# Where the bias table fills stand in an encoder layer: from the windowed attention into the first FFN's gate/up blocks

## The chip, the cores and the metric

The kernel runs on one core of a Trainium2 chip. The metric is the device time of one execution in microseconds (us). The kernel before takes 2405.37 us, the median of three runs (2403.84 to 2407.05).

## The reference

One encoder layer with two half-step SwiGLU FFNs around a mixing layer. The mixing layer has two kinds of heads: A, windowed grouped-query attention with rotary embedding (rope), and B, a neighbourhood attention on a token grid, whose scores get a learned relative position bias from the table `rpb_b`, and minus infinity (-1e30) where a key lies outside the neighbourhood. There are 1024 sample tokens and 256 prompt tokens, D_MODEL = 1024, D_FF = 2816.

```python
def swiglu(x, w_gu, w_down):
    g, u = jnp.split(x @ w_gu, 2, axis=-1)
    return (jax.nn.silu(g) * u) @ w_down
...
def encoder_layer(x, ffn1_pre, ffn1_w_gu, ffn1_w_down, ffn1_post, mix_pre, w_in, sink_a, rpb_b,
                  out_norm_a, out_norm_b, w_out, mix_post, ffn2_pre, ffn2_w_gu, ffn2_w_down, ffn2_post, final_norm):
    B, S, _ = x.shape
    x = x + 0.5 * rmsnorm(swiglu(rmsnorm(x, ffn1_pre), ffn1_w_gu, ffn1_w_down), ffn1_post)
    h = rmsnorm(x, mix_pre)
    proj = h @ w_in
    qa, ka, va, qb, kb, vb = jnp.split(proj, np.cumsum([D_A, D_KV_A, D_KV_A, D_B, D_B]), axis=-1)
    qa = rope(qa.reshape(B, S, N_HEADS_A, HEAD_DIM))
    ka = rope(ka.reshape(B, S, N_KV_A, HEAD_DIM))
    va = va.reshape(B, S, N_KV_A, HEAD_DIM)
    oa = window_gqa(qa, ka, va, sink_a)
    ob = neighbourhood_attn(qb.reshape(B, S, N_HEADS_B, HEAD_DIM), kb.reshape(B, S, N_HEADS_B, HEAD_DIM),
                            vb.reshape(B, S, N_HEADS_B, HEAD_DIM), rpb_b)
    mix = jnp.concatenate([rmsnorm(oa, out_norm_a), rmsnorm(ob, out_norm_b)], axis=-1) @ w_out
    x = x + rmsnorm(mix, mix_post)
    x = x + 0.5 * rmsnorm(swiglu(rmsnorm(x, ffn2_pre), ffn2_w_gu, ffn2_w_down), ffn2_post)
    return rmsnorm(x, final_norm)
```

## The kernel before

**Stages.** The 1280 tokens are 10 tiles of 128. The stages follow one another on TensorE: gate/up of the first FFN (to about 608 us), its down product (to about 900 us), the input projections, attention A, attention B, the output projection, the second FFN, the final norm. Every product is made of three matmuls over a high and a low part of each operand (`ah`, `al` for weights; `xh`, `xl` for activations).

**Gate/up** is in class `GateUp`. D_FF is cut into NFF = 22 blocks of 128, HF = 11 in each half. A block f is 14 steps: 7 products over a chunk of 256 columns and 7 over a chunk of 384, the 7 being the products of a Strassen scheme, each with its own weight operand. Step n is number n of these 14. `run(f)` issues the steps of block f, and between them `prep(f + 1)`, which makes the seven operand pairs A(f+1) (`ah` on ScalarE, L69; `al` and the sums `s` on VectorE, L72 and L249 to L258) from the raw weights. At its end `load(f + 2)` (L229) loads the raw weights raw(f+2), two loads of 512 KB, on SP's queue. The raw tiles have two buffers, so one pair: raw(f+2) needs raw(f+1) to have been used up. The results `w` and `v` of a block are stored to HBM on ACT's queue (`store`, L319) and, in the second half, the planes of the first half are read back by `fetch` (L326) on SP's queue. `weight_sums` loads `bx` and `bt` of the down weights (L396 to L401) on SP, adds them on GpSimd (POOL) and stores them (`td0T`) on ACT's queue.

**Bias tables.** `bias_tables` makes the tables `tt` and `ttp` in HBM that attention B reads as `tab`. A *skew* loads `cm` (L538), adds rows of `rpb_b` to it on GpSimd (`z`) and stores it to the scratch tensors `zd` and `zp` (L544). `fill_neg` writes 512 KB of minus infinity to `ttp` (L564). A *fill* is one HBM to HBM DMA `tt<-zd` of 384 KB (L552) and one or two DMAs `tt<-in_neg_dram` of 48 to 192 KB (L557), whose source is one short row of minus infinity read for every row of the target. `fill_p` is four DMAs `ttp<-zp` (L560). There are six skews, 16 fills and four `fill_p`. In the kernel before, hook 6 of blocks 2 to 10 takes the first nine pieces (six skews, the first fill, then two fills at a time), tied behind the last raw weight load by `issue_after`; the rest goes as the list `fills` to attention A, where `pinned` ties each behind the latest rope swap.

**Attention A** runs four groups j of heads. While group j runs, the queries of group j+1 are projected and go through `rope`: the projection is copied to `qf`, four DMAs on SP's queue swap its halves into `qs` (L709), and `qf`, `qs` are multiplied and added (L711 to L714). The scores need the split operand of it (`stk`).

**Order.** The instructions of each engine, and the DMAs of each queue, run in the order of the built program; a scheduler sets this order at build, within the ties of `issue_after`. A DMA also waits until the DMA that last used its completion semaphore has landed; eight such semaphores go round among the DMAs of SP and ACT.

Of the kernel before, what the change touches and what calls it, by code (L numbers as in the profile page):

```python
# [32 lines left out]
HF = NFF // 2  # L33
# [133 lines left out]
class GateUp:  # L167
# [8 lines left out]
    def __init__(self, c, tc, w_gu, wp, G, hd):  # L176
        self.c, self.tc, self.wp, self.G, self.hd = c, tc, wp, G, hd
        self.w = w_gu.rearrange("(k p) (s f) -> p k s f", p=128, s=2)
        self.xb = [[None] * 7 for _ in CHUNKS]
        self.A, self.raw, self.back, self.later, self.held, self.last_v = {}, {}, {}, [], [], []  # L180
        self.work = None

# [41 lines left out]
    def load(self, f):  # L224
        if f < NFF:
            self.raw[f] = []
            for s in range(2):
                r = self.wp.tile([128, 8, 128], F32, name="raw", bufs=2)
                self.last_load = self.c.nc.sync.dma_start(r, self.w[:, :, s, f * 128:(f + 1) * 128])  # L229
                self.raw[f].append(r)  # L230
# [90 lines left out]
    def fetch(self, f, ch):  # L321

        n = CN[ch]
        x = self.back[f, ch] = self.G.tile([128, 2 * n], F32, name="back", tag="x", bufs=3)
        with self.tc.issue_after(self.last_load.ins):
            self.c.nc.sync.dma_start(x.rearrange("p (r x) -> p r x", x=128), self.plane(("w0", "v0"), f, ch))  # L326

# [18 lines left out]
    def steps(self, f):  # L346
        k = "01"[f >= HF]

        def step(ch, j):
            self.product(f, ch, j)  # L350
            if j == 0:
                self.queued(self.last_v)
            if j == 4:
                self.queued(self.later)
# [163 lines left out]
def bias_tables(c, G, rpb, cmask, neg, tt, ttp, zd, zp):  # L518
# [4 lines left out]
    nc = c.nc  # L523
# [44 lines left out]
    fills = [lambda a=a, rh=rh: fill(a, rh) for a in range(8) for rh in range(2)][1:]  # L568
    while len(first) < HF - 2:
        two, fills = fills[:2], fills[2:]  # L570
        first.append(lambda two=two: [f() for f in two])
    return first, fills + [lambda a=a: [fill_p(a, n) for n in range(4)] for a in range(4)]

# [27 lines left out]
def mix_attention(c, tc, xt, w_in, sink, cosT, sinT, maskA, tt, ttp, oAd, oBd, mw, L, R,  # L601
                  close_left, open_out, late, mr, pre, fills):
    nc = c.nc
# [98 lines left out]
    def rope(th, ps, store):  # L702
# [5 lines left out]
        for b in range(4):  # L708
            state["pin"] = nc.sync.dma_start(qs[b * 32:b * 32 + 32], qf[(b ^ 1) * 32:(b ^ 1) * 32 + 32])  # L709
        yield  # L710
# [38 lines left out]
    qA = {}  # L749
# [211 lines left out]

    def pinned(f):
        with tc.issue_after(state["pin"].ins):
            f()

    with in_order(tc, mybir.EngineType.DVE):
# [11 lines left out]
    for j in range(4):  # L978
        units = [[(att_A(j, t), ATT)] for t in range(NT)]
        if j < 3:  # L980
            todo = P(("qA", j + 1))
            for n in range(7):
                if fills:
                    todo.insert(4 * n + 3, (0.0, lambda f=fills.pop(0): pinned(f)))
            pipe.run(units, todo)
        else:
            pipe.run(units + [[]] * 5, P(("qkB", 0), ("vB", 1)))
# [183 lines left out]
def encoder(tc, i, out_p, out_s):  # L1171
# [206 lines left out]
    gu.load(2)  # L1378
    late, later = bias_tables(c, G, i["rpb_b"][0], i["cmask"], i["neg"], tt, ttp, zd, zp)

    def behind():
        with tc.issue_after(gu.last_load.ins):
            late.pop(0)()

    for f in range(1, NFF):
        gu.run(f, block_hooks(gu, f, {6: behind} if 1 < f < HF else {}, f // 2 if f == 1 or f % 2 == 0 else None))
    L.close(2)
# [30 lines left out]
    def finish1(t, x, gain, halves, ss):  # L1418
# [7 lines left out]
        if "xt" in state:  # L1426
# [7 lines left out]
            else:  # L1434
# [9 lines left out]
    mix_attention(c, tc, state["xt"], i["w_in"][0], i["sink_a"], i["cosT"], i["sinT"], i["maskA"], tt, ttp, oAd, oBd,  # L1444
                  mw, L, R, lambda: L.close(4), mo.open, lambda: [list(x) for x in state["late"]], state["mr"], state["pre"], later)
    c.ps.use(y=(2, 3, 4, 5), tr=(6, 7, 0, 1))
# [64 lines left out]
    def finish2(t, x, gain, halves, ss):  # L1511
# [8 lines left out]
        for h in (a, b):  # L1520
            nc.scalar.dma_start(rows(ys, yp, t)[:, h], x[:, h])

# [53 lines left out]
```

## Time and profile before

The profiled execution took 2403.19 us; its span, from the first to the last instruction, is 2401.4 us.

| | before |
|---|---|
| median of three runs | 2405.37 us |
| the profiled execution | 2403.19 us |
| its span | 2401.4 us |
| PE (TensorE) busy | 2273.8 us, 95% |
| VectorE, ScalarE, POOL busy | 1458.6, 982.4, 709.0 us |
| mean granted TensorE clock | 0.977 of full speed |
| HBM traffic | 372.47 MB, mean 155 GB/s |

The profile's rows name an engine, a line of the kernel, an operation and out<-in by the program's names. SPq and ACTq are the queues on which these engines issue DMAs. A row of waits says which engine waited at which line for which instruction: us in total, times, longest. The granted clock is the share of full speed at which TensorE ran. The busy share is 95% over the whole span, so it has to be read stage by stage.

### The profile page before, as it was taken

What the parts mean: (1) busy time and instruction counts of PE and PEld (TensorE: products, weight loads), DVE (VectorE), ACT (ScalarE), POOL (GpSimd) and SP (SyncE); (2) the same over time, 40 slices, a digit from 0 to 9 for tenths busy, and PEclk for the clock granted to TensorE, in tenths of its full rate; (3) what the DMA queues carried; (4) which work ended last, traced back from release to release, by engine and by line L of the source; (5) the groups of instructions that cost most, each with busy time, mean ns of one, the idle gap of its engine ahead of it and who ended that gap; (6) DMA issues with size and microseconds to landing.
All of it is one profiled execution on the core that took longest, in us unless ns stands there. A gap on an engine that the chain in (4) does not pass through costs nothing. (4 is left out here: it accounts for less than half of the span.)

```text
span 2401.4 us, 36895 instructions
## 1 busy us (share of the span) xinstructions
PE 2273.8 (95%) x13328; PEld 2072.3 (86%) x13328; DVE 1458.6 (61%) x2575; ACT 982.4 (41%) x2043; POOL 709.0 (30%) x812
## 2 busy tenths in 40 slices
PE   6999999999999999878999989899999999999997
PEld 5999999999788787657898878789999999978876
DVE  7666656655545763548665656566666656544585
ACT  5322222222434543547665655342322222243454
POOL 6121125444000123436443334622213332300022
PEclk9999999999999999878999999899999999999999
DMA  4466656666656653334433445435455655555574
GB/s 135 119 155 158 153 144 195 188 184 185 208 188 192 221 184 107 73 77 85 111 106 93 123 156 176 155 114 164 139 172 157 185 145 159 149 189 183 191 230 157
DMA packets 417094, 372.47 MB, mean 155 GB/s; under 512 B 69200, under 2 KB 339408, under 8 KB 416912
## 3 DMA queue, kind: packets, MB, share of 16 engines
q1 hardware_dynamic: 286224, 278.87, 39.5%
q10 hardware_dynamic: 130688, 91.25, 12.4%
q8 instruction: 105, 1.72, 0.3%
q14 instruction: 77, 0.63, 0.1%
HBM read 249.85 MB, written 121.90 MB: 155 GB/s over the span
## 5 line engine op out<-in xcount | busy, mean ns | idle before, releaser
L280 PE MATMUL gups<-xh,ah 128*128 128x256 f32 (+1 forms) x2464 | 764.9, 311 | 18.6 <-DVE v L289 13.5
L280 PE MATMUL gups<-xh,al 128*128 128x256 f32 (+1 forms) x2464 | 762.1, 310 | 0.0
L280 PE MATMUL gups<-xl,ah 128*128 128x256 f32 (+1 forms) x2464 | 761.8, 309 | 0.0
L462 PE MATMUL dps<-wd,hh 128*128 128x512 f32 x1540 | 482.4, 394 | 7.9 <-ACT hh L69 7.9
L280 PEld LDWEIGHTS gups<-xh,ah 128*128 128x128 f32 x2464 | 466.7, 189 | 24.5 <-DVE v L289 15.8
L280 PEld LDWEIGHTS gups<-xl,ah 128*128 128x128 f32 x2464 | 467.3, 190 | 0.0
L280 PEld LDWEIGHTS gups<-xh,al 128*128 128x128 f32 x2464 | 466.9, 190 | 0.0
L462 PEld LDWEIGHTS dps<-wd,hh 128*128 128x128 f32 x1540 | 290.9, 189 | 70.3 <-ACT hh L69 9.8
L462 PE MATMUL dps<-wd,hl 128*128 128x512 f32 x770 | 304.2, 395 | 6.6 <-DVE hl L72 6.2
L69 ACT ACTIVATE ah<-s 128x512 fp32r<-128x512 f32 x176 | 111.3, 632 | 244.4 <-PE gups L280 165.9
L72 DVE TENSOR_TENSOR al<-s,ah 128x512 fp32r<-128x512 f32 x176 | 145.0, 824 | 98.1 <-ACT ah L69 97.4
L69 ACT ACTIVATE hh<-hl 128x768 fp32r<-128x768 f32 (+1 forms) x140 | 110.6, 791 | 209.6 <-DMA hl<-hd0s 55.3
L72 DVE TENSOR_TENSOR hl<-hl,hh 128x768 fp32r<-128x768 f32 (+1 forms) x140 | 124.6, 891 | 106.3 <-ACT hh L69 106.3
L462 PEld LDWEIGHTS dps<-wd,hl 128*128 128x128 f32 x770 | 145.8, 189 | 44.2 <-DVE hl L72 12.6
L659 POOL TENSOR_TENSOR sb<-sb,rc 128x384 f32<-128x384 f32 (+1 forms) x160 | 126.1, 810 | 158.0 <-DVE rc L657 144.3
L636 PE MATMUL pj<-xh,mh 128*128 128x512 f32 (+1 forms) x432 | 162.9, 378 | 0.3
L636 PE MATMUL pj<-xh,ml 128*128 128x512 f32 (+1 forms) x432 | 156.8, 363 | 0.1
L636 PE MATMUL pj<-xl,mh 128*128 128x512 f32 (+1 forms) x432 | 156.3, 362 | 0.0
L306 ACT ACTIVATE u<-u 128x256 f32<-128x256 f32 x88 | 41.5, 472 | 253.4 <-DVE u L289 208.9
L69 ACT ACTIVATE ah<-raw 128x512 fp32r<-128x512 f32 x132 | 83.4, 632 | 138.4 <-PE gups L280 131.5
L72 DVE TENSOR_TENSOR wd<-rawd,wd 128x512 fp32r<-128x512 f32 x154 | 106.2, 692 | 47.0 <-ACT wd L69 46.5
L162 POOL TENSOR_SCALAR rs<-ssq 128x1 f32<-128x1 f32 x20 | 12.5, 624 | 396.1 <-ACT junk L479 396.1
(183 smaller groups left out, 3680.4 us busy)
## 6 DMA issues: line engine op xcount, KB each, us to landing
raw<-in_ffn_w_gu_dram SPq DMA_DIRECT2D x88, 512.0 KB, 4.1
rawd<-in_ffn_w_down_dram SPq DMA_DIRECT2D x66, 256.0 KB, 3.3
bx<-in_ffn_w_down_dram SPq DMA_DIRECT2D x22, 512.0 KB, 5.1
bt<-in_ffn_w_down_dram SPq DMA_DIRECT2D x44, 256.0 KB, 4.8
rawd<-td0T SPq DMA_DIRECT2D x44, 256.0 KB, 3.2
rawd<-td1T SPq DMA_DIRECT2D x44, 256.0 KB, 3.2
tab<-tt SPq DMA_DIRECT2D x24, 384.0 KB, 3.8
hl<-hd0s SPq DMA_DIRECT2D x20, 384.0 KB, 3.2
```

What stands on the lines that cost most here:

```text
L69: nc.scalar.activation(hi, src, AF.Copy)
L72: (lo_eng or nc.vector).tensor_tensor(lo, src, hi.bitcast(F32), op=ALU.subtract)
L162: nc.gpsimd.tensor_scalar(r, sums[0], sums[1] if len(sums) == 2 else 0.0, EPS, op0=ALU.add, op1=ALU.add)
L280: nc.tensor.matmul(ps, w[:, k, :], x[:, k, :], start=new and k == 0 and m == 0, stop=k == 3 and m == 2, skip_group_check=not new)
L306: self.last_act = nc.scalar.activation(X["u"], X["u"], AF.Silu)
L462: nc.tensor.matmul(ps, a[:, k, :], b, start=i == 0 and v == 0, stop=i == HF - 1 and v == 2)
L636: state["mm"] = nc.tensor.matmul(ps[:, :n], w[:, kk, :], xs[th][:, kk, :], start=first, stop=last)
L659: nc.gpsimd.tensor_tensor(s, s, rc[:, i:i + 1].to_broadcast(list(s.shape)), op=ALU.mult)
```

## The change

Four things change.

1. All pieces of the bias tables are queued in the first FFN: hooks 6 and 12 of blocks 2 to 10 take a piece each, none is left for attention A, and `pinned` goes.
2. A read-back by `fetch` now also counts as the last load, and each raw weight load is tied behind the last load, so raw loads are queued behind the values read back.
3. The queued stores of `later` are issued at step 5, not 4, of a chunk.
4. The output stores of the last norm go on SP's queue, not ACT's.

```diff
@@ GateUp.load
-                self.last_load = self.c.nc.sync.dma_start(r, self.w[:, :, s, f * 128:(f + 1) * 128])
+                with self.tc.issue_after(self.last_load.ins) if self.last_load else nullcontext():
+                    self.last_load = self.c.nc.sync.dma_start(r, self.w[:, :, s, f * 128:(f + 1) * 128])
@@ GateUp.fetch
-            self.c.nc.sync.dma_start(x.rearrange("p (r x) -> p r x", x=128), self.plane(("w0", "v0"), f, ch))
+            self.last_load = self.c.nc.sync.dma_start(x.rearrange("p (r x) -> p r x", x=128), self.plane(("w0", "v0"), f, ch))
@@ GateUp.steps
-            if j == 4:
+            if j == 5:
                 self.queued(self.later)
@@ bias_tables
     fills = [lambda a=a, rh=rh: fill(a, rh) for a in range(8) for rh in range(2)][1:]
-    while len(first) < HF - 2:
+    fills += [lambda a=a: [fill_p(a, n) for n in range(4)] for a in range(4)]
+    while fills:
         two, fills = fills[:2], fills[2:]
         first.append(lambda two=two: [f() for f in two])
-    return first, fills + [lambda a=a: [fill_p(a, n) for n in range(4)] for a in range(4)]
+    return first
@@ mix_attention
-            todo = P(("qA", j + 1))
-            for n in range(7):
-                if fills:
-                    todo.insert(4 * n + 3, (0.0, lambda f=fills.pop(0): pinned(f)))
-            pipe.run(units, todo)
+            pipe.run(units, P(("qA", j + 1)))
...
     def behind():
-        with tc.issue_after(gu.last_load.ins):
-            late.pop(0)()
+        if late:
+            with tc.issue_after(gu.last_load.ins):
+                late.pop(0)()
 
     for f in range(1, NFF):
-        gu.run(f, block_hooks(gu, f, {6: behind} if 1 < f < HF else {}, f // 2 if f == 1 or f % 2 == 0 else None))
+        gu.run(f, block_hooks(gu, f, {6: behind, 12: behind} if 1 < f < HF else {}, f // 2 if f == 1 or f % 2 == 0 else None))
@@ finish2
         for h in (a, b):
-            nc.scalar.dma_start(rows(ys, yp, t)[:, h], x[:, h])
+            nc.sync.dma_start(rows(ys, yp, t)[:, h], x[:, h])
```

**SP's queue in the first FFN.** Before, this is all that stands from the raw pair of block 10 (first row) to that of block 11 (last row):

```order
L229 DMA raw<-in_ffn_w_gu_dram 128x8x128 x2
L552 DMA tt<-zd 16x24x256
L557 DMA tt<-in_neg_dram 16x24x128
L552 DMA tt<-zd 16x24x256
L557 DMA tt<-in_neg_dram 16x24x128
L229 DMA raw<-in_ffn_w_gu_dram 128x8x128 x2
```

Now this stands between the raw pair of block 7 and that of block 8 (line numbers of the changed kernel are one to two higher; `x2` is two such DMAs):

```order
L553 DMA tt<-zd 16x24x256
L558 DMA tt<-in_neg_dram 16x24x32
L558 DMA tt<-in_neg_dram 16x24x96
L553 DMA tt<-zd 16x24x256
L558 DMA tt<-in_neg_dram 16x24x128
L397 DMA bx<-in_ffn_w_down_dram 128x1024
L401 DMA bt<-in_ffn_w_down_dram 128x512
L402 DMA bt<-in_ffn_w_down_dram 128x512
L553 DMA tt<-zd 16x24x256
L558 DMA tt<-in_neg_dram 16x24x64 x2
L553 DMA tt<-zd 16x24x256
L558 DMA tt<-in_neg_dram 16x24x128
```

Four fills stand there in place of two at most. Between raw pairs 8 and 9 there are again four fills with six `tt<-in_neg_dram`, without `bx` and `bt`; between 9 and 10 four fills with six, and `bx`, `bt`, `bt`; between 6 and 7 three `tt<-zd` and three `tt<-in_neg_dram`; between 10 and 11 one fill with one and twelve of the sixteen `ttp<-zp`. Of the skews, two stand in blocks 2, 3 and 4 each, where before one stood in blocks 2 to 7.

**VectorE at the edge of a block.** Before, at the edge of blocks 7 and 8 (`128x384` is the last chunk of block 7, `128x256` the first of block 8):

```order
L72 TENSOR_TENSOR al<-s_2632,ah 128x512
L303 TENSOR_TENSOR w<-w,g 128x384
L289 TENSOR_TENSOR u<-u,gups 128x384
L72 TENSOR_TENSOR al<-raw,ah 128x512
L249 TENSOR_TENSOR s_2880<-raw 128x512
L307 TENSOR_TENSOR v<-v,u 128x384
L250 TENSOR_TENSOR s_2881<-s_2880,raw 128x512
L289 TENSOR_TENSOR u<-u,gups 128x256
```

Now, at the same edge:

```order
L290 TENSOR_TENSOR u<-u,gups 128x384
L308 TENSOR_TENSOR v<-v,u 128x384
L72 TENSOR_TENSOR al<-raw,ah 128x512
L250 TENSOR_TENSOR s_2652<-raw 128x512
L251 TENSOR_TENSOR s_2653<-s_2652,raw 128x512
L72 TENSOR_TENSOR al<-s_2653,ah 128x512
L72 TENSOR_TENSOR al<-raw,ah 128x512
L255 TENSOR_TENSOR s_2653<-raw,s_2653 128x512
L72 TENSOR_TENSOR al<-s_2652,ah 128x512
L290 TENSOR_TENSOR u<-u,gups 128x256
```

Before, the first operand of A(9) and two of its sums stood there, and A(8), whose last row is the first one shown, had been made among the products of block 7. Now all of A(8) from its first operand on stands behind block 7's products, and four of the seven ahead of block 8's first product (`u<-u,gups 128x256` reads that).

**SP's queue in attention A**, for j = 1, before and now:

```order
L709 DMA qs<-qf 32x512 x4
L799 DMA oAd<-st 64x2x128
L552 DMA tt<-zd 16x24x256
L557 DMA tt<-in_neg_dram 16x24x32
L557 DMA tt<-in_neg_dram 16x24x96
L799 DMA oAd<-st 64x2x128
L552 DMA tt<-zd 16x24x256
L557 DMA tt<-in_neg_dram 16x24x128
L709 DMA qs<-qf 32x256 x4
```

```order
L711 DMA qs<-qf 32x512 x4
L801 DMA oAd<-st 64x2x128 x2
L711 DMA qs<-qf 32x512 x3
L801 DMA oAd<-st 64x2x128
L711 DMA qs<-qf 32x512
```

The rope swaps `qs<-qf` follow one another with only the small stores `oAd<-st` between.

More of the change, by code (lines that the diff above doesn't have):

```diff
@@ L1 @@
 import math
-from contextlib import contextmanager
+from contextlib import contextmanager, nullcontext
 import numpy as np
@@ L180, in __init__ @@
         self.A, self.raw, self.back, self.later, self.held, self.last_v = {}, {}, {}, [], [], []
-        self.work = None
+        self.work = self.last_load = None
     def open_chunk(self, ch, pool):
@@ L601, in mix_attention @@
 def mix_attention(c, tc, xt, w_in, sink, cosT, sinT, maskA, tt, ttp, oAd, oBd, mw, L, R,
-                  close_left, open_out, late, mr, pre, fills):
+                  close_left, open_out, late, mr, pre):
     nc = c.nc
@@ L708, in rope @@
         for b in range(4):
-            state["pin"] = nc.sync.dma_start(qs[b * 32:b * 32 + 32], qf[(b ^ 1) * 32:(b ^ 1) * 32 + 32])
+            nc.sync.dma_start(qs[b * 32:b * 32 + 32], qf[(b ^ 1) * 32:(b ^ 1) * 32 + 32])
         yield
@@ L960, in P @@
         return out
-    def pinned(f):
-        with tc.issue_after(state["pin"].ins):
-            f()
     with in_order(tc, mybir.EngineType.DVE):
@@ L1378, in encoder @@
     gu.load(2)
-    late, later = bias_tables(c, G, i["rpb_b"][0], i["cmask"], i["neg"], tt, ttp, zd, zp)
+    late = bias_tables(c, G, i["rpb_b"][0], i["cmask"], i["neg"], tt, ttp, zd, zp)
     def behind():
-        with tc.issue_after(gu.last_load.ins):
-            late.pop(0)()
+        if late:
+            with tc.issue_after(gu.last_load.ins):
+                late.pop(0)()
     for f in range(1, NFF):
-        gu.run(f, block_hooks(gu, f, {6: behind} if 1 < f < HF else {}, f // 2 if f == 1 or f % 2 == 0 else None))
+        gu.run(f, block_hooks(gu, f, {6: behind, 12: behind} if 1 < f < HF else {}, f // 2 if f == 1 or f % 2 == 0 else None))
     L.close(2)
@@ L1444, in encoder @@
     mix_attention(c, tc, state["xt"], i["w_in"][0], i["sink_a"], i["cosT"], i["sinT"], i["maskA"], tt, ttp, oAd, oBd,
-                  mw, L, R, lambda: L.close(4), mo.open, lambda: [list(x) for x in state["late"]], state["mr"], state["pre"], later)
+                  mw, L, R, lambda: L.close(4), mo.open, lambda: [list(x) for x in state["late"]], state["mr"], state["pre"])
     c.ps.use(y=(2, 3, 4, 5), tr=(6, 7, 0, 1))
```

## The prediction

> **What bounds the kernel now.** I read first the table of stretches (each row: from and to, length, then busy us of PE, PEld, DVE, ACT and POOL with instructions, then PE's granted clock, the DMA share and GB/s), because a busy share over the whole span hides where TensorE stands still.
>
> ```profile
> 77.00:322.00 245.00, 244.66 (x1681) 244.32 (x1680) 152.25 (x251) 68.71 (x130) 38.29 (x29) 1.00 0.59 148
> 322.00:608.00 286.00, 272.96 (x1845) 269.43 (x1844) 169.77 (x272) 74.26 (x143) 124.26 (x109) 0.99 0.64 185
> 956.00:1116.00 160.00, 122.45 (x606) 99.89 (x605) 93.93 (x257) 85.91 (x228) 71.88 (x126) 0.82 0.35 79
> 1116.00:1380.00 264.00, 261.08 (x1637) 231.45 (x1636) 174.20 (x485) 174.01 (x467) 109.23 (x161) 1.00 0.39 105
> ```
>
> Row 1 is blocks 1 to 10 of the first FFN's gate/up stage, 168 matmuls each, so 24.46 us a block: TensorE is full, at full clock, and nothing can be gained there, only lost. Row 3 is attention A for j = 0 to 2, the one stage where TensorE is starved: 37.6 us idle, and a clock of 0.82 in the rest. Row 4, the rest of the attention, is full again.
>
> Then the waits of the engines, in those two stages (us in total, times, longest). The first row is TensorE's only wait in row 1 above; the other three are in row 3.
>
> ```profile
> PE gups L280 <- DVE v L289: 0.3, 1, 0.3
> PE o_ps L792 <- DVE st L687: 14.2, 8, 3.6
> PE s_ps L665 <- DVE stk L72: 12.9, 7, 3.3
> ACT stk L69 <- DVE qf L714: 26.1, 10, 5.1
> ```
>
> In attention A the scores (`s_ps`) wait for `stk`, ScalarE waits for `qf` before it can make `stk`, and `qf` needs `qs`, the rotated half that the rope fetches by a DMA on SP's queue. So I looked at that queue where a bias fill stands ahead of a rope swap. First the timeline of SP (start, issue time, instruction), then the DMA view of single issues (KB each, us from issue to landing).
>
> ```profile
> 1011.77 0.60 SPq L552 DMA_DIRECT2D tt<-zd  x1
> 1012.41 1.28 SPq L557 DMA_DIRECT2D tt<-in_neg_dram  x2
> 1014.46 0.60 SPq L552 DMA_DIRECT2D tt<-zd  x1
> 1015.11 0.62 SPq L557 DMA_DIRECT2D tt<-in_neg_dram  x1
> 1015.82 10.09 SPq L709 DMA_DIRECT2D qs<-qf  x4
> ...
> tt<-zd SPq DMA_DIRECT2D x1, 384.0 KB, 4.0
> tt<-in_neg_dram SPq DMA_DIRECT2D x1, 48.0 KB, 8.9
> tt<-in_neg_dram SPq DMA_DIRECT2D x1, 144.0 KB, 13.8
> tt<-zd SPq DMA_DIRECT2D x1, 384.0 KB, 13.8
> tt<-in_neg_dram SPq DMA_DIRECT2D x1, 192.0 KB, 17.9
> qs<-qf SPq DMA_DIRECT2D x1, 32.0 KB, 17.4
> qs<-qf SPq DMA_DIRECT2D x3, 32.0 KB, 1.8
> ```
>
> Issue plus landing gives the chain: 1015.8 (table rows from `zd`), 1021.3 (fill with minus infinity, 48 KB), 1026.9 (144 KB), 1028.3 (`zd`, 384 KB), 1033.0 (192 KB), 1033.2 (the swap). The reader is to see two things. The queue lands in order, so the swap took 17.4 us where three others with no fill ahead (issued at 961 us) took 1.8. And a `tt<-in_neg_dram` **holds the queue for 4.7 to 5.6 us whatever its size**, while a `tt<-zd` with up to eight times the bytes takes 1.4. The fill's source is one row read over and over. I use 5.3 and 1.4.
>
> **The change: attention A loses its fills.** Busy 122.45 us at clock 0.82 is 100.4 us of work at full speed, so 160 - 100.4 = 59.6 us is all that this stage can give. What it keeps is read from two 20 us stretches: the stage's first, and the first of j = 3, which runs attention A without fills and without rope.
>
> ```profile
> 956.00:976.00 20.00, 16.78 (x76) 13.44 (x75) 16.65 (x41) 13.27 (x33) 11.68 (x18) 0.83 0.26 69
> 1016.00:1036.00 20.00, 11.69 (x58) 8.94 (x58) 10.18 (x29) 8.78 (x23) 7.61 (x14) 0.72 0.26 77
> 1116.00:1136.00 20.00, 19.11 (x113) 15.47 (x113) 17.53 (x50) 16.44 (x46) 14.18 (x27) 0.97 0.43 96
> ```
>
> The start stays 20 us: its 16.78 x 0.83 = 13.9 us of work waits for the first softmax chains as well. The other 86.5 us of work at the pace of j = 3 (19.11 / 20 x 0.97 = 0.927) take 93.3 us. So 160 becomes 113.3: **a gain of 46.7 us**. From above it is bounded by 59.6. From below: if only the waits of `s_ps` go (12.9 of the 37.6 us idle), and with them as large a share of the 22.1 us that the low clock costs (122.45 - 100.4), it is 12.9 + 7.6 = 20.5.
>
> **The change: the fills go to blocks 5 to 10 of the first FFN.** On DVE, ACT and POOL they cost nothing, since a fill is DMA alone. On SP they stand between two pairs of raw weight loads. The sixteen fills are 16 `tt<-zd` and 22 `tt<-in_neg_dram`. By the order shown above, six of the latter stand between raw(7) and raw(8), six up to raw(9) and six up to raw(10); the kernel before has at most three between two pairs. The rows of a stretch with one or two fills in the kernel before:
>
> ```profile
> 271.53 0.58 SPq L552 DMA_DIRECT2D tt<-zd  x1
> 272.54 0.56 SPq L557 DMA_DIRECT2D tt<-in_neg_dram  x1
> 307.31 0.62 SPq L557 DMA_DIRECT2D tt<-in_neg_dram  x1
> 307.97 3.09 SPq L396 DMA_DIRECT2D bx<-in_ffn_w_down_dram  x1
> ...
> tt<-zd SPq DMA_DIRECT2D x1, 384.0 KB, 4.5
> tt<-in_neg_dram SPq DMA_DIRECT2D x1, 192.0 KB, 8.8
> tt<-in_neg_dram SPq DMA_DIRECT2D x1, 192.0 KB, 14.0
> bx<-in_ffn_w_down_dram SPq DMA_DIRECT2D x1, 512.0 KB, 15.1
> ```
>
> `zd` lands at 276.0 and the fill behind it at 281.3: 5.3 us here too. The other fill lands at 321.3 and `bx`, 512 KB, at 323.1: 1.7 us for a plain load of that size, so 3.4 for a pair of raw loads and about the same, 3.4, for `bx` with its two halves `bt`. The stretches then take, on the queue alone:
> raw(7) to raw(8): 6 x 5.3 + 4 x 1.4 + 3.4 + 3.4 = 44.2 us; raw(8) to raw(9): 6 x 5.3 + 4 x 1.4 + 3.4 = 40.8; raw(9) to raw(10): 44.2. Against three blocks of 24.46 that is 19.7 + 16.3 + 19.7 = **55.7 us**.
>
> Is there cover? There is one pair of raw buffers, so raw(f+2) is loaded only after A(f+1) has been made from raw(f+1). Below are SP's waits from 77 to 345 us.
>
> ```profile
> SPq L229 <- DVE s L258: 69.5, 10, 18.8
> SPq L538 <- DMA td0T<-bt: 36.3, 4, 12.3
> SPq L229 <- DVE al L72: 23.1, 9, 3.2
> SPq L544 <- POOL z L542: 22.0, 5, 5.0
> SPq L557 <- DMA hd0w<-w: 9.1, 1, 9.1
> SPq L552 <- DMA hd0w<-w: 8.8, 1, 8.8
> ```
>
> SP waits 69.5 + 23.1 us over some eleven pairs, 8.4 us a block, for the raw buffer: that idle time hides what stands between the loads today. It would shorten the first long stretch. I do not subtract it from the sum, because of the last two rows: a fill waits until the DMA that used its completion semaphore before has landed, here a store of products by ACT. With four fills per block many wait for stores of the very block that they run beside, and the queue stands empty meanwhile. The cover stays in the lower bound, 55.7 - 8.4 = 47.
>
> The skews before the fills double up too: two in one block where one stood. Each costs SP about 9.1 us (36.3 / 4) at L538 and 4.4 (22.0 / 5) at L544; two are 27 us in a block of 24.46, and with the raw loads 30.4. In two such blocks (4 and 5) that is 2 x 6 = 12 us, less a little of the cover: 11, between nothing and 27 (one added skew in each, uncovered).
>
> Behind a wait of 15 to 20 us the clock is low: 0.72 in the stretch from 1016 us, that is 5.6 us of 20. While the queue sets the pace this is hidden; for block 10, behind which it no longer does, I take 4 us (0 to 6). The Trainium skill ("TensorE: Matmul & The Clock Gate", section "What's actually happening") says that the clock is halved after an idle window of about 3.4 us and restored after as long a busy one; by it one such wait would cost about 1.7 us, an estimate from that page, in place of my 4, and the sum would be 2 us less.
>
> Sum of the first FFN: 11 + 55.7 + 4 = **+71 us**, from 47 (skews and clock at nothing) to 27 + 55.7 + 6 + 6 = 95, the last 6 for stores that the queue waits for.
>
> Behind the cover stands one more lateness, which DVE's order shows: the seven operands of A(f+1) stand at the edge of the block, behind block f's own work, and the first step of the block waits for them.
>
> **The change: the rest.** In four blocks of the second half and in one of FFN2 the first of the two raw loads now stands behind `back`, not ahead of it. The place where that is longest:
>
> ```profile
> 469.87 0.38 SPq L229 DMA_DIRECT2D raw<-in_ffn_w_gu_dram  x1
> 474.80 0.38 SPq L326 DMA_DIRECT2D back<-hd0w  x1
> ```
>
> That raw load goes out 4.9 us later or less, and the second one no later. The idle 13 us of that stage (286.00 - 272.96) are not waits for raw weights, so nothing is won; what is lost I put at +1 (0 to 4.9, one full delay). The hook moved from j = 4 to 5 leaves every order as it was: 0. The output stores on SP's queue in place of ACT's: 20 stores of 256 KB beside other loads, in a stage where TensorE is busy 263.69 of 268 us:
>
> ```profile
> 2120.00:2388.00 268.00, 263.69 (x1136) 214.21 (x1137) 160.13 (x231) 124.28 (x222) 23.07 (x34) 0.99 0.62 198
> ```
>
> The stores free some time of ACT's queue and may hold up a weight load behind them; the stage's idle 4.3 us bounds a gain, a like amount a loss: 0 +- 4.
>
> **Sum.** The profiled execution took 2403.2 us (span 2401.4 and 1.8 around it). 2403.2 + 71 + 1 - 46.7 = 2428.5. It lies 2.2 below the median of the runs, 2405.4, so in those terms I say **2430 us**.
>
> **The rivals.**
> (a) *The fills are hidden beside TensorE.* Row 1 has a DMA share of 0.59, so there is room, if a fill in a full queue costs what its bytes do: by `bx` (1.7 us for 512 KB) 0.2 to 0.6 us, and no stretch exceeds 12.4 + 6 x 0.6 = 16 us. It decides at (24.46 + 8.4 - 12.4) / 6 = 3.4 us per fill: below that, nothing is lost. Only the gain would be left: 2405.4 - 46.7 + 1 = **2360 us, faster**. Against it: four fills in two stages took 4.7 to 5.6 us, with queued loads right behind. The Trainium skill ("DMA: Bandwidth & Descriptors", section "Measured (HBM→SBUF, 128 partitions, SWDGE, issued from GpSimd)") has 0.95 us for 64 KB and 6.15 for 1 MB, an estimate of 1.6 for 192 KB and so of 22 for a stretch, which would side with (a); the trace, with 5.3 us, differs. Chance 0.10.
> (b) *Both bounds meet*: loss 47 and gain 50 to 59.6, so 2394 to 2403. Speaks for it that the cover is real. Chance 0.08.
> (c) *Attention A is held by the rope itself.* `o_ps` waits 14.2 us for `st`, not for a swap; if only the 12.9 us of `s_ps` are gained, the time is 2405.4 + 72 - 12.9 = **2464 us**. Against it: j = 3 and the 1.8 us swaps. Chance 0.12.
> (d) *The change doesn't do what it says*: the scheduler could leave fills in the attention. SP's order there shows none. Chance 0.
>
> **How the numbers follow.** The forecast has 0.70, between 2404 and 2462 with its terms. The range takes in (b) and (c) and leaves (a) out: 2394 to 2466. A measurement of this kernel can tell about 0.2%, 4.8 us, from no change. Faster: (a) and half of (b), 0.14. Within: the other part of (b) and the forecast's lower edge, 0.07. Slower: 0.79.
>
> **What would show it.** In the changed profile, blocks 7 to 9 should last 40 to 45 us each, with TensorE waiting at their start for `ah` or `al` made from raw weights, raw landings of 10 us and more, and six fills landing 5 us apart ahead of each pair. Attention A to j = 2 should last about 113 us at a clock over 0.9, its swaps landing in about 2 us. I am wrong if the FFN's blocks stay at 24.5 us, or if the swaps are fast and the scores still wait for `stk`.

## The result, and the profile after

| | before | after |
|---|---|---|
| median of four runs | 2404.61 us (2402.42 to 2407.05) | 2438.09 us (2434.73 to 2443.76) |
| ratio, with its 95% interval | | 1.0141 (1.0119 to 1.0163) |
| the profiled execution, its span | 2403.19, 2401.4 us | 2439.03, 2437.3 us |
| blocks 7, 8, 9 of the first FFN together | 73.3 us | 138.4 us |
| start of block 11 | 322.5 us | 408.9 us |
| first FFN's down product, first to last matmul | 282.2 us | 283.0 us |
| attention A, first to last score | 195.1 us | 137.0 us |

The change costs 1.4%. The forecast was 2430, within 2394 to 2466. A block starts here with its first `gups` matmul in the trace.

The windows of the changed kernel, columns as in the prediction (from and to, length, PE, PEld, DVE, ACT, POOL busy, clock, DMA share, GB/s). Rows 1 to 4 are blocks 7 to 10, row 5 is attention A:

```profile
241.40:282.80 41.40, 25.25 (x169) 24.27 (x168) 14.66 (x27) 6.96 (x14) 5.22 (x4) 0.87 0.43 119
282.80:327.20 44.40, 27.95 (x169) 27.21 (x169) 13.98 (x26) 6.43 (x13) 0.00 (x0) 0.81 0.37 97
327.20:379.80 52.60, 28.03 (x168) 27.08 (x168) 14.20 (x25) 6.43 (x13) 5.35 (x4) 0.76 0.51 122
379.80:408.90 29.10, 28.39 (x169) 27.95 (x170) 13.99 (x26) 5.91 (x12) 0.00 (x0) 0.85 0.61 122
1047.00:1187.00 140.00, 133.61 (x841) 116.88 (x840) 125.12 (x357) 115.81 (x323) 104.74 (x180) 0.98 0.28 60
```

The three blocks hold the same 168 matmuls as ever, in 41 to 53 us: TensorE stands still for a third to a half of each and restarts at a low clock. In attention A it is now busy for 133.6 of 140 us at 0.98. The DMA share falls where the loss is (0.43 and 0.37 beside 0.59 before): the transfers are not short of bandwidth, something keeps them from being issued or from landing.

The waits of the changed kernel say what (engine, line, waited for: us, times, longest). The first row is TensorE's and the middle ones SP's, from 78 to 410 us; the last row is TensorE's in attention A:

```profile
PE gups L281 <- ACT ah L69: 57.2, 6, 21.8
...
SPq L230 <- DMA td0T<-bt: 30.7, 2, 16.6
SPq L558 <- DMA hd0w<-w: 18.8, 2, 13.6
SPq L230 <- DMA hd0w<-w: 16.1, 1, 16.1
SPq L553 <- DMA hd0w<-v: 13.8, 1, 13.8
...
PE s_ps L667 <- DVE stk L72: 3.4, 2, 2.4
```

TensorE waits 57.2 us for `ah`, the first operand of the next block. SP has two kinds of trouble: transfers that land slowly, and waits for stores by ACT (`td0T<-bt`, `hd0w<-w`, `hd0w<-v`: the four rows in the middle, 79.4 us) that must land before a DMA gets its completion semaphore. In the forecast's sum the second kind stands at nothing, with 6 us in its upper bound; what such a wait costs is not its length, as block 8 shows. Scores hardly wait for `stk` any more: 3.4 us where it was 12.9.

Both kinds are seen in block 8. First SP's timeline (start, issue time, instruction) of the changed kernel, then its DMA view of single issues there (KB, us to landing):

```profile
289.00 0.55 SPq L558 DMA_DIRECT2D tt<-in_neg_dram  x1
303.36 0.54 SPq L553 DMA_DIRECT2D tt<-zd  x1
303.94 0.63 SPq L558 DMA_DIRECT2D tt<-in_neg_dram  x1
...
310.29 17.12 SPq L230 DMA_DIRECT2D raw<-in_ffn_w_gu_dram  x2
...
tt<-in_neg_dram SPq DMA_DIRECT2D x1, 192.0 KB, 15.7
tt<-zd SPq DMA_DIRECT2D x1, 384.0 KB, 4.8
tt<-in_neg_dram SPq DMA_DIRECT2D x1, 192.0 KB, 9.2
raw<-in_ffn_w_gu_dram SPq DMA_DIRECT2D x1, 512.0 KB, 16.2
```

SP issues nothing from 289.6 to 303.4: the wait of 13.8 us for the store `hd0w<-v` above. But the queue does not run dry meanwhile: the 192 KB issued at 289.00 land only at 304.7, 15.7 us after their issue, behind four DMAs issued from 283.6 on. The `zd` of 303.36 lands at 308.2, the 192 KB of minus infinity behind it at 313.1 (4.9 us later), and so on until the first raw load, issued at 310.3, lands at 326.5. Block 9 starts at 327.2.

By the issue and landing times of all its DMAs, SP's queue has nothing under way for 2.5 of the 138.4 us of the three blocks. So the work on the queue sets their pace, as the forecast had it. An estimate of what a wait of SP costs there is the restart of the queue: the `tt<-zd` issued at 258.2, with nothing ahead of it, landed after 3.6 us, where one behind others takes 1.4 by the prediction's chain.

Where the 35.9 us between the spans come from, by the block and stage starts of the two traces: block 6 starts 16.7 later (skews; 1.4 of it stand already at block 1), blocks 7 to 9 take 65.0 more, block 10 takes 4.6 more, block 11 to the down product 2.9 more, the down product 0.8 more; attention A takes 58.1 less; FFN2's down product and the tail take 3.4 more. That is 35.3, so nothing large is missing.

### The profile page after: what moved, and what is told of

Read it like the earlier page. It is cut to its first block, busy times and chain, and to the rows that moved or that the text cites. A ratio compares the mean times of both kernels' runs of the same rounds, so it can differ in the third digit from the quotient of the medians.

```text
span 2437.3 us, 36888 instructions
## 1 busy us (share of the span) xinstructions
PE 2263.7 (93%) x13328; PEld 2068.8 (85%) x13328; DVE 1447.9 (59%) x2575; ACT 975.1 (40%) x2043; POOL 714.0 (29%) x812
## 5 line engine op out<-in xcount | busy, mean ns | idle before, releaser
L281 PEld LDWEIGHTS gups<-xh,ah 128*128 128x128 f32 x2464 | 473.3, 192 | 98.8 <-ACT ah L69 63.4
L281 PEld LDWEIGHTS gups<-xh,al 128*128 128x128 f32 x2464 | 473.1, 192 | 1.9 <-DVE al L72 1.9
L281 PEld LDWEIGHTS gups<-xl,ah 128*128 128x128 f32 x2464 | 473.8, 192 | 0.0
L72 DVE TENSOR_TENSOR al<-s,ah 128x512 fp32r<-128x512 f32 x176 | 139.3, 791 | 107.1 <-ACT ah L69 106.1
L307 ACT ACTIVATE u<-u 128x256 f32<-128x256 f32 x88 | 41.4, 471 | 290.2 <-DVE u L290 236.5
L403 POOL TENSOR_TENSOR bt<-bt,bx 128x512 f32<-128x512 f32 x22 | 30.3, 1377 | 419.4 <-DMA bt<-in_ffn_w_down_dram 352.3
```

Of the source, the lines that this page charges most:

```text
L72: (lo_eng or nc.vector).tensor_tensor(lo, src, hi.bitcast(F32), op=ALU.subtract)
L281: nc.tensor.matmul(ps, w[:, k, :], x[:, k, :], start=new and k == 0 and m == 0, stop=k == 3 and m == 2, skip_group_check=not new)
L307: self.last_act = nc.scalar.activation(X["u"], X["u"], AF.Silu)
L403: e(b22, b22, b12, op=sub)
```

## The experiments

Every kernel ran beside the kernel before on the same chip; a ratio is against those runs. Lengths are from the profiled execution of each, which lies up to 7.7 us from the median of its kernel.

| kernel | median us | ratio (95%) | blocks 7-9 | block 11 starts | down product | attention A |
|---|---|---|---|---|---|---|
| fills_only | 2438.48 | 1.0146 (1.0123 to 1.0169) | 137.2 | 411.0 | 284.9 | 134.9 |
| rest_only | 2413.09 | 1.0029 (1.0016 to 1.0042) | 73.8 | 325.5 | 287.4 | 193.6 |
| skews_only | 2423.23 | 1.0072 (1.0055 to 1.0090) | 73.9 | 341.5 | 284.0 | 195.0 |
| after_own_rows | 2409.63 | 1.0014 (1.0005 to 1.0023) | 99.8 | 379.0 | 284.8 | 135.2 |
| before_own_rows | 2409.06 | 1.0009 (1.0000 to 1.0018) | 73.4 | 325.4 | 284.3 | 191.9 |
| fills_in_down | 2390.26 | 0.9934 (0.9910 to 0.9959) | 73.4 | 323.4 | 321.9 | 137.1 |
| small_copies_in_A | 2393.84 | 0.9945 (0.9930 to 0.9960) | 73.8 | 323.7 | 325.4 | 137.3 |
| large_copies_in_A | 2461.80 | 1.0228 (1.0213 to 1.0244) | 73.4 | 324.5 | 324.3 | 205.3 |
| fills_in_A_written_order | 2400.43 | 0.9970 (0.9959 to 0.9981) | 73.3 | 323.5 | 283.2 | 183.3 |
| fills_in_down_wider | 2380.23 | 0.9887 (0.9872 to 0.9902) | 74.1 | 323.6 | 314.9 | 136.9 |
| small_copies_in_ffn | 2404.97 | 0.9991 (0.9979 to 1.0004) | 74.4 | 328.8 | 313.5 | 136.0 |
| large_copies_in_ffn | 2457.10 | 1.0208 (1.0190 to 1.0225) | 101.4 | 373.2 | 310.1 | 135.8 |

### Which part of the change costs

`fills_only` is the kernel before with the bias pieces moved and nothing else of the change (the lists of `bias_tables`, hooks 6 and 12, no `pinned`).

> The kernel before with the fills' part of the change alone (all pieces in blocks 2 to 10, none in attention A); raw loads, output stores and the hook at step 4 as before. Theory (the fills make the loss of the first FFN and the gain of attention A; raw order and output stores cost about 3 us each): the first FFN's gate/up stage ends 84 to 88 us later than before, attention A is 56 to 60 us shorter, together 2404.6 + 27 to 30 = 2431 to 2435 us. Rival (the raw loads tied behind the read-back make a good part of the loss): below 2425 us.

`rest_only` is the other half: the raw loads tied behind `back`, `later` at step 5, the output stores on SP.

> The kernel before with everything of the change but the fills: raw loads behind the read-back, the hook at step 5, output stores on SP's queue. Theory: the first FFN's second half is about 3 us longer, the last down product and the tail about 3 us: 2404.6 + 4 to 8 = 2409 to 2413 us. Rival (these edits cost nothing by themselves, the 3 us came from the shifted state after the fills): 2403 to 2406 us.

`skews_only` doubles only the skews, in blocks 2 to 4; the later hooks are as before.

```diff
-        gu.run(f, block_hooks(gu, f, {6: behind} if 1 < f < HF else {}, ...
+        gu.run(f, block_hooks(gu, f, ({6: behind, 12: behind} if 1 < f < 5 else {6: behind} if 7 < f < HF else {}), ...
```

> The kernel before with one thing of the change: the six skews stand two to a block in blocks 2 to 4 (hooks 6 and 12) and not one to a block in 2 to 7; the fills as before. Theory (16.7 us of the loss of the first FFN come from the skews, ahead of any fill): block 6 starts 12 to 18 us later than before, the blocks behind it last 24.5 us, attention A as before, 2417 to 2426 us. Rival (the early loss in the changed kernel comes from the fills that follow in block 5): below 2411 us.

The moved pieces alone give the whole net loss (2438.48, 3.5 us above what was expected). The rest costs 6 us by itself (2413.09 beside 2406.97). FFN2's down product has a part of it: 278.4 to 279.2 us in the three kernels with the output stores on SP, 274.9 to 276.5 in the others. Block 11 to the down product takes 292.3 us beside 287.3, but that is not shown to come from the raw loads: it takes 290.3 in `fills_only` too, where they stand as before. Single profiles differ by such amounts also where no edit reaches: the first FFN's down product takes 282.2 to 287.4 us in the eight kernels that leave it as it was. The parts do not add up to the us, since `fills_only` and the full change have the same time. The doubled skews put block 6 back by 18.5 us, nearly all the 16.7 of the changed kernel.

### Is it the one row that is read over and over?

A scratch tensor `nd` is filled once with minus infinity, 192 KB, and every `tt<-in_neg_dram` reads it instead, each target row from a source row of its own. The bytes, the queue and the places are the same.

```diff
-                src = bass.AP(tensor=neg.tensor, offset=neg.offset, ap=[[0, 16], [0, 24], [1, n]])
-                nc.sync.dma_start(tf[:, :, a, rh, lo * 32:hi * 32], src)
+                nc.sync.dma_start(tf[:, :, a, rh, lo * 32:hi * 32], nd[:, :, :n])
```

> The changed kernel, but the 22 DMAs that write minus infinity to tt read it from a scratch tensor nd of 16 x 24 x 128 in which every row of the source is a row of its own (written once, by one more DMA, ahead of block 1); same number, size and place of the DMAs, nearly the same order on every engine. Theory (such a DMA holds SP's queue for 5.3 us because all its 384 rows read the same short row): it takes 0.5 to 1.6 us, raw(8) to raw(10) follow one another in 24 to 28 us, blocks 7 to 9 last 24.5 to 29 us and not 41 to 53, and the time falls by 50 to 65 us to 2373 to 2388. Rival 1 (what costs is the order that was made at build, with A(f+1) at the edge of the block): blocks stay above 33 us, above 2410. Rival 2 (what costs is the writing of 384 short rows): each still takes 5 us, 2435 to 2441.

> The kernel before, with the 22 DMAs of minus infinity reading the same scratch tensor nd, rows of their own; the fills stay where they were, 13 of them in attention A. Theory: the rope swaps behind a fill land 2 to 5 us after their issue and not 9 to 17, and of the 58 us that attention A lost in the kernel before 35 to 55 come back: 2350 to 2370 us, with the first FFN at its old 24.5 us a block. Rival (any fill ahead of a swap holds attention A, by its waits on SP for the ties behind the swaps): less than 20 us come back, above 2385.

In the changed kernel with own rows (`after_own_rows`), SP's timeline and then the DMA view of these two issues:

```profile
312.99 0.58 SPq L555 DMA_DIRECT2D tt<-zd  x1
313.63 0.61 SPq L559 DMA_DIRECT2D tt<-nd  x1
...
tt<-zd SPq DMA_DIRECT2D x1, 384.0 KB, 5.3
tt<-nd SPq DMA_DIRECT2D x1, 192.0 KB, 5.2
```

`zd` lands at 318.3 and `nd` at 318.8: 0.5 us for what took 4.9. So the 5 us are the price of one short row read 384 times, not of a DMA from HBM to HBM. With all eighteen of them in blocks 7 to 9 freed of it, the three blocks should have come close to 24.5 us each. The windows of the same kernel say otherwise, and under them are its waits from 248 to 380 us (TensorE) and 195 to 380 us (SP):

```profile
248.40:278.10 29.70, 25.20 (x169) 24.23 (x167) 15.60 (x27) 6.96 (x14) 5.45 (x4) 1.00 0.53 151
278.10:311.50 33.40, 28.29 (x168) 27.28 (x168) 13.86 (x25) 6.33 (x13) 0.00 (x0) 0.85 0.48 129
311.50:348.20 36.70, 27.56 (x169) 26.66 (x169) 14.00 (x27) 6.44 (x13) 5.62 (x4) 0.90 0.56 163
...
PE gups L281 <- ACT ah L69: 21.0, 6, 5.2
...
SPq L555 <- DMA hd0w<-w: 36.5, 4, 11.0
```

They take 99.8 us, 26.4 over three full blocks, and the expectation of 2373 to 2388 us failed (2409.63). Without the repeated row 38.6 of the 65.0 us in these blocks go, and 29.9 of the delay of block 11. The 26.4 us are not a share that the queue's work left over in the changed kernel: there the queue was empty for 2.5 of 138.4 us, here it is empty for 38.2 of 99.8. With the row reads gone, a second limit shows that was hidden behind them. It goes with SP's waits for stores and with TensorE's wait for `ah` at each edge.

The stores tell the two kernels apart. Below are those of `w`, from issue to landing (median), first in the changed kernel (180 to 410 us), then with own rows (195 to 380 us):

```profile
hd0w<-w ACTq DMA_DIRECT2D x7, 192.0 KB, 11.7
...
hd0w<-w ACTq DMA_DIRECT2D x6, 192.0 KB, 2.1
```

In the changed kernel ACT's stores land late themselves, while the one row is read on SP's queue. With own rows they land soon, but ACT issues them late: the `zd` that SP issues at 333.1 waited for a store issued at 331.3.

In the attention the same edit is worth 3 us: `before_own_rows` has its fills there, swaps that land in 2 to 4 us, and an attention A of 191.9. The expectation of 2350 to 2370 failed, and with it the reason that the prediction gave for the gain.

### What holds the attention, if not the swap's landing

`fills_in_down` takes the own rows and issues the fifteen pieces of the list `fills` (eleven fills and the four `fill_p`; the expectation counts 13 fills) in the first FFN's down product, one at every second of its steps from step 22. `small_copies_in_A` is the same, with fifteen pairs of copies of 6 KB tied behind the swaps where the fills stood; `large_copies_in_A` makes these copies 192 KB. The copies go to a scratch tensor that nothing reads.

```diff
+    def beneath(f):
+        with tc.issue_after(gu.down.last_h.ins):
+            f()
-    down_phase(..., {60: open_xt, 64: first_split})
+    down_phase(..., {22 + 2 * n: lambda f=f: beneath(f) for n, f in enumerate(later)} | {60: open_xt, 64: first_split})
...
+        nc.sync.dma_start(tt2[:, :, a % 4, :4], ndd[0][:, :, :4])
+        nc.sync.dma_start(tt2[:, :, a % 4, 128:128 + 4], ndd[0][:, :, :4])
```

(The last two lines are those of the small copies; the large ones have 128 for each 4 that is a width.)

> The kernel before with the 13 fills and four fill_p of attention A put into the down product of the first FFN (one piece every second step from step 22, behind the latest load of h), reading minus infinity from a scratch tensor with rows of its own, which is written once ahead of the first fill; gate/up, raw loads and output stores as before. Theory (what attention A loses is lost by fills being there at all, the gate/up loss by four fills a block): attention A takes 136 to 141 us and not 195, the gate/up stage its old time within 4 us, the down product 0 to 8 us more: 2347 to 2362 us, below both kernels. Rival (attention A is shorter only in the shifted state behind the long first FFN): above 2385 us.

> The kernel with the fills in the down product, and beside that, in attention A where the fills stood, 15 pieces of two DMAs each on SP's queue, tied behind the rope swaps as the fills were, that copy 16 x 24 x 4 elements between scratch tensors that nobody reads. The order at build is as without them: projection, scores and values alternate on TensorE. Theory (attention A loses by the order that is made at build when large DMAs stand in SP's queue; TensorE's projections run ahead in bunches): attention A takes 137 to 145 us, within 8 us of the kernel without them. Rival (DMAs between the swaps and the stores of SP cost by their number, their issue and their semaphores): 160 us or more in attention A, 20 us or more slower than without them.

> The same with 16 x 24 x 128 elements a copy (192 KB, rows of their own): same number, same ties; at build this makes nearly the order of the kernel before, with the projections in bunches. Each copy should land 0.5 to 1.5 us behind the one ahead of it. Theory (order): attention A takes 180 to 195 us as in the kernel before, though no swap waits over 5 us for its landing, 2395 to 2412 us in all. Rival (the time that the queue is held): 30 copies of 0.5 to 1 us are 15 to 30 us, of which TensorE sees part: attention A 140 to 160 us, 2350 to 2380 us.

Attention A in four kernels, one row of the windows and SP's wait for `st` there: before; before with own rows, with TensorE's wait for `stk`; small copies; large copies. With small copies SP's longest wait is another, 19.4 us for `pl` at the same store.

```profile
959.10:1154.20 195.10, 158.80 (x838) 131.18 (x839) 125.22 (x355) 117.92 (x321) 95.98 (x176) 0.85 0.35 78
SPq L799 <- DVE st L687: 38.5, 12, 7.5
```

```profile
966.10:1158.00 191.90, 154.94 (x838) 127.07 (x839) 125.06 (x355) 117.58 (x321) 95.86 (x175) 0.88 0.34 79
SPq L800 <- DVE st L688: 67.8, 10, 20.4
PE s_ps L666 <- DVE stk L72: 13.0, 6, 3.3
```

```profile
1010.20:1147.50 137.30, 131.97 (x838) 115.56 (x839) 122.98 (x354) 114.25 (x320) 101.53 (x176) 0.99 0.31 59
SPq L802 <- DVE st L690: 9.3, 6, 3.2
```

```profile
1009.10:1214.40 205.30, 159.63 (x838) 129.78 (x839) 125.06 (x355) 117.95 (x321) 96.47 (x175) 0.85 0.26 66
SPq L802 <- DVE st L690: 99.6, 15, 20.7
```

`fills_in_down` has the gain of the attention (137.1), but not the 2347 to 2362 us expected: its down product takes 39.7 us more, and not up to 8. Thirty copies in the queue of the attention cost it nothing if they are small, and 68 us if they are large (205.3, above the 180 to 195 expected), though the DMA share is lower with the large ones (0.26 beside 0.31). What differs is where SP stands: with large copies it waits 99.6 us for `st` (L690) at the attention's small store `oAd<-st`, with small ones 9.3. Whatever is queued behind that store, the swaps too, waits with it. That this wait is what holds the stage, and not itself a result of a stage held elsewhere, the rows do not show.

The trace of one rope shows it. The view by tile, of `qf`, first in `before_own_rows` with SP's timeline behind it, then in the changed kernel (first and last start in us):

```profile
L707 ACT ACTIVATE qf<-pj x2: 384/482/581, 988.0 to 1003.3; 128x512 f32<-128x512 f32 x1, 128x256 f32<-128x256 f32 x1
L710 SPq DMA_DIRECT2D qs<-qf x8: 560/589/594, 1007.8 to 1024.1; - x8
L712 POOL TENSOR_TENSOR qf<-qf,cos x2: 1254/1258/1261, 999.1 to 1027.1; 128x512 f32<-128x512 f32 x2
L715 DVE TENSOR_TENSOR qf<-qf,qs x2: 692/692/693, 1000.4 to 1028.4; 128x512 f32<-128x512 f32 x2
...
1005.79 0.60 SPq L800 DMA_DIRECT2D oAd<-st  x1
1007.79 2.46 SPq L710 DMA_DIRECT2D qs<-qf  x4
```

```profile
L708 ACT ACTIVATE qf<-pj x2: 375/484/592, 1072.6 to 1080.7; 128x512 f32<-128x512 f32 x1, 128x256 f32<-128x256 f32 x1
L711 SPq DMA_DIRECT2D qs<-qf x8: 564/582/1201, 1073.2 to 1083.0; - x8
L716 DVE TENSOR_TENSOR qf<-qf,qs x2: 674/674/675, 1069.8 to 1082.5; 128x512 f32<-128x512 f32 x2
```

With the fills in the attention, `qf` is written at 988.0, but its swap is issued at 1007.8, behind a store at 1005.8. It has landed at 1011.8, yet POOL's product with `cos` (L712) starts at 1027.1, behind softmax work, and the sum of the rope comes at 1028.4. Of these 40 us 20 pass ahead of the issue, 4 in the landing, and 16 behind it. Without the fills the swap follows `qf` within 0.6 us, and the sum comes 10 us after it (1072.6 to 1082.5). So the rope stands later on POOL as well, and not on SP's queue alone. These orders were made at build; the same lines of code, with nothing but the size of a copy changed, give another order.

Is TensorE's order enough to mend it? `fills_in_A_written_order` keeps the fills in the attention, with own rows, and holds TensorE there to the order in which the code is written:

```diff
+    with in_order(tc, mybir.EngineType.PE):
+        for j in range(4):
```

> The kernel before with the fills left where they stand, in attention A (minus infinity from rows of its own, written once in block 8), and TensorE's instructions of attention A held to the order in which the code is written, so that projection, scores and values alternate again; SP's order keeps its fills, and the rope swaps stand behind fills and behind the stores of the output as before. Theory in its narrow form (TensorE's bunched order makes the loss of attention A): it takes 137 to 155 us and not 195, 2350 to 2370 us, faster than any kernel so far. Rival (what the order does on SP makes it: the swaps stand behind stores that wait for the softmax): 175 us or more, 2390 us or more.

Attention A takes 183.3 us, so no. Its window, and SP's wait there:

```profile
966.30:1149.60 183.30, 143.99 (x853) 125.53 (x854) 127.29 (x354) 115.43 (x320) 97.53 (x177) 0.92 0.37 85
SPq L802 <- DVE st L690: 60.2, 15, 12.7
```

SP still waits 60.2 us at that store. Which other order does it (SP's own, POOL's, VectorE's, ScalarE's) was not tried apart, and stays open.

### The same question in the FFN

`fills_in_down_wider` spreads the pieces further in the down product, at every third step from step 6 (`{6 + 3 * n: ...}`). On it, `small_copies_in_ffn` and `large_copies_in_ffn` add ten copies to each of blocks 5 to 10, five at hook 6 and five at hook 12, of 6 KB or 192 KB, from own rows into scratch that nothing reads:

```diff
+    def copies(a):
+        with tc.issue_after(gu.last_load.ins):
+            for n in range(5):
+                nc.sync.dma_start(tt2[:, :, (5 * a + n) % 8, :4], nd2[:, :, :4])
```

> The kernel with the fills in the down product of the first FFN (minus infinity from rows of its own), now one piece every third step from step 6 in place of every second from step 22. There the down product took 322 us and not 282, with TensorE waiting for h behind the fills on SP's queue. If that is a matter of how densely the pieces stand, the down product takes 285 to 305 us and the whole 2352 to 2375 us; if each piece costs its 2.3 us wherever it stands in that stage, it stays at 2387 to 2394 us. Attention A 137 us and gate/up as before in both.

> The same kernel, and beside it in blocks 5 to 10 of the first FFN's gate/up, at hooks 6 and 12, five DMAs each on SP's queue behind the last raw load (ten a block, as many as the changed kernel's four fills have), that copy 16 x 24 x 4 elements between scratch tensors that nobody reads. At build A(f+1) stays among the products of block f. Theory (what the changed kernel loses beside the hot row and the skews, some 25 to 30 us, comes from the order made at build, with A(f+1) at the edge of the block): blocks 6 to 10 last 24.5 to 26 us, the first block of the second half starts within 8 us of the kernel without copies. Rival (it comes from the number of DMAs between two raw loads, whose semaphores make them wait for ACT's stores): blocks of 28 us and more.

> The same with 16 x 24 x 128 elements a copy (192 KB, rows of their own); at build A(f+1) then stands at the edge of the block from block 6 on, as in the changed kernel. Each copy holds the queue for 0.5 to 1 us, ten a block 5 to 10 us, so the queue alone has room in 24.5 us. Theory (order): blocks 6 to 10 last 29 to 37 us as in the changed kernel with rows of its own, 30 to 60 us more than with small copies. Rival (only the queue's time counts): 24.5 to 26 us a block.

The windows of blocks 7 to 10 with small copies, then of blocks 7 to 9 with large ones, each with the thirty copies that the DMA view shows there, and for the large ones TensorE's wait:

```profile
230.00:328.80 98.80, 98.21 (x673) 97.60 (x673) 55.87 (x96) 25.37 (x49) 7.25 (x5) 1.00 0.59 139
tt<-nd SPq DMA_DIRECT2D x30, 6.0 KB, 3.6
```

```profile
229.30:330.70 101.40, 80.47 (x504) 77.80 (x504) 42.57 (x76) 19.21 (x39) 11.83 (x9) 0.90 0.60 161
tt<-nd SPq DMA_DIRECT2D x30, 192.0 KB, 3.8
PE gups L280 <- ACT ah L69: 17.8, 5, 12.6
```

With thirty small copies these four blocks take 98.8 us, 24.7 a block: TensorE is full. (The kernel as a whole is 25 us slower than `fills_in_down_wider`, mostly in block 6, which takes 30.0 us, and from block 11 on.) The large ones land as fast (3.8 us beside 3.6) and have no repeated row, yet three blocks take as long as four. In VectorE's built order, what stands behind blocks 6 to 8 is as in the kernel before where the copies are small; where they are large it is as in the changed kernel (the operands of A(f+1) behind the products of block f), and so on to block 11. With small copies that late order first stands behind block 11, and blocks 11 and 12 are the slow ones, 38.8 and 35.1 us. So about 28 us in blocks 7 to 9 (101.4 less three of 24.46) come with large DMAs in the queue without any repeated row, as the 26.4 did in `after_own_rows`. SP's waits for stores do not do it alone: with small copies there are some of up to 12.2 us while TensorE is full. Nor does VectorE's order: 12.6 of TensorE's 17.8 us above are one wait, ahead of block 8, whose first raw load landed at 267.5. It was issued at 261.1, behind four copies that SP could not issue before a store had landed at 258.3. How much each has in all, these runs do not part.

`fills_in_down_wider` beats both kernels: 2380.23 us, 1.1% under the kernel before. It keeps the gain of the attention and pays 32.7 us in the down product (314.9 beside 282.2), less than the 39.7 of `fills_in_down` and more than its expectation. TensorE's waits there, before and in this kernel:

```profile
PE dps L462 <- ACT hh L69: 2.3, 1, 2.3
```

```profile
PE dps L462 <- ACT hh L69: 18.9, 7, 3.6
```

TensorE waits for `hh`, which ScalarE makes from the values that SP loads (`hl`), and the pieces stand between these loads on SP's queue. These waits are 16.6 of the 32.7 us. A still wider spread was not tried.

## Why the prediction was right, and where its steps failed

Sign and size came out: +33.5 us between the medians, where 24.6 was forecast. Both large terms were too small, by 15.4 us (loss to block 11) and 11.4 us (attention), and set each other off, which was luck. The likeliest case was the one that happened, by its sum; by its mechanism, half of it.

| step of the prediction | forecast | measured | what the runs showed |
|---|---|---|---|
| doubled skews | +11 | +16.7 | alone 18.5; the step was mis-sized, within its bounds of 0 and 27 |
| three stretches of raw loads | +55.7 | +65.0 | the queue empty for 2.5 of 138.4 us; with own rows 26.4 stay, by another limit |
| half clock in block 10 | +4 | +4.6 | right in size |
| raw loads behind `back` | +1 | +2.9 | 3.0 in `fills_only`, without this edit: not shown to be theirs |
| output stores | 0 +- 4 | +3.4 | FFN2's down product 2.3, the tail 1.1 |
| attention A | -46.7 | -58.1 | gain real, its reason wrong |

**The stretches.** The sum on the queue alone, "6 x 5.3 + 4 x 1.4 + 3.4 + 3.4", held for the changed kernel. Its unit was 5 us after the change as before, the queue was hardly ever empty, and the first raw loads of the three pairs landed 20.0, 16.2 and 22.1 us after their issue, as the signs said (10 us and more). By blocks the forecast was 44.2, 40.8 and 44.2, the trace has 41.4, 44.4 and 52.6. The term that was mis-sized is the raw pair: in the last block its two loads took 4.5 and 4.0 us of landings and not 3.4 together, and the first of them could be issued only after a store of ACT had landed (327.0).

The step that failed is what the prediction put behind the queue: waits of fills for ACT's stores, and operands that stand at the block's edge in VectorE's order. Both were named and not priced, but for 6 us for stores in the upper bound. With 0.5 us in place of 5.3 the same sum gives 15.4 us for the first stretch, less than a block's 24.46, so with own rows no loss should have been left; 26.4 us were.

**Rival (a)**, fills that hide beside TensorE, needed less than 3.4 us per `tt<-in_neg_dram`. With own rows that holds, and still the blocks grew by 26.4. So (a) would have failed even where its condition was met: its decision point left out the order and the waits for stores.

**The attention.** The step that failed is "The queue lands in order, so the swap took 17.4 us", as the cause of the idle TensorE. The swaps did land late; but when they land in 2 to 4 us, as in `before_own_rows`, the scores wait for `stk` as before (13.0 us beside 12.9). Fast swaps beside waiting scores are the sign that the prediction had named for being wrong. With the fills there the built order is another: swaps behind a store that waits for `st`, and the rope's products late on POOL; which part of it holds the stage is open. That is closer to **rival (c)**, the rope holding the attention, than to the forecast, but (c) priced the gain at 12.9 us, taking the order for fixed. The size came right because it was read from j = 3, a stretch with neither fills nor rope, whatever the reason; where it was off is the pace: it was taken at 0.927 with the first 20 us left as they were, and came out 1.5 us short of the bound of 59.6.

**The clock.** Two restarts in the windows of the changed kernel, blocks 8 and 10, and the wait inside the second in TensorE's timeline:

```profile
282.80:286.00 3.20, 3.16 (x13) 2.94 (x13) 0.69 (x1) 0.00 (x0) 0.00 (x0) 0.51 0.90 229
379.80:388.20 8.40, 7.69 (x33) 7.38 (x34) 5.34 (x9) 1.94 (x4) 0.00 (x0) 0.50 0.77 133
...
383.76 0.58 PE L281 MATMUL gups<-xh,ah 128*128 128x256 f32 x1 [0.69 <-ACT ah L69]
```

Behind the wait ahead of block 8 TensorE worked 3.2 us at half clock, which costs 1.6; behind the one ahead of block 10 it was 8.4 us, which costs 4.2 of the 4.6. The Trainium skill ("TensorE: Matmul & The Clock Gate", section "What's actually happening") has full speed back after a busy window of about 3.4 us. The first restart agrees. The second took 4.6 us from the end of the short wait inside it (383.76 to 388.4). The clock changes of this trace lie whole multiples of 3.41 us apart (the half clock from 361.0 to 388.3 is eight of them), and this half clock ends with the first such stretch without a wait of TensorE, 384.9 to 388.3; whether the wait of 0.69 us before it is the reason was not tested. The 4 us of the forecast was nearer than the single window of the Trainium skill, but the row that it was read from, 0.72 in the stretch from 1016 us, is not behind a wait of 15 to 20 us: the longest wait of TensorE in that attention is 3.6 us.

## What to carry to other kernels

When DMAs are moved in a kernel that a scheduler orders, compare the built order of every engine around both places before pricing queue time: here the same copies at 6 KB and at 192 KB gave an attention of 137 and of 205 us with landings alike. Price a DMA by how its source is read and not by its bytes alone: one short row read for every target row cost 5 us where rows of its own cost 0.5. And test a cause by taking away only it: a size that comes out right does not show that its reason was, and what stays may be a second limit that the first had hidden.

## What the runs showed of the hardware

A DMA whose source is one short row read 384 times held its queue for about 5 us whether it moved 48 or 192 KB; 192 KB from 384 different rows took 0.5. While that row was read on SP's queue, stores of 192 KB on ACT's queue landed late too, after 11.7 us (median) beside 2.1 without it. Beside the raw loads, thirty copies of 6 KB in four blocks cost TensorE next to nothing there (24.7 us a block). And a queue can be slow while it moves little: the blocks with the longest waits have DMA shares of 0.37 to 0.51, less than the full blocks' 0.59.
